# HGRN2 beside token projections: order of its small matmuls, banks of the projections, and norms of two banks at a time

## The chip, the cores and the metric

The kernel runs on one core of one Trainium2 chip, in one launch. The metric is the device time of an execution in microseconds (us); lower is better. Three runs of the kernel before were timed, and one further execution was profiled.

## The reference

A decoder trunk of two layers over 512 tokens of width 1024, all in float32. Each layer is a half-step SwiGLU, a mixing block and another half-step SwiGLU, each behind an RMS norm and added to the stream:

```python
for l in range(DEPTH):
    x = x + 0.5 * swiglu(rms_norm(x, ffn1_norm[l]), ffn1_w_in[l], ffn1_w_out[l])
    h = rms_norm(x, mix_norm[l]) @ w_mix_in[l]
    (c_x, c_b, c_c, h_q, h_f, h_i, h_g, f_q, f_k, f_v, f_f) = jnp.split(h, split_at, axis=-1)
    y = jnp.concatenate([
        short_conv_mixer(c_x, c_b, c_c, conv_w[l]),
        hgrn2_mixer(h_q, h_f, h_i, h_g, lower_bounds[l], hgrn_out_gain[l]),
        fox_mixer(f_q, f_k, f_v, f_f, fox_f_bias[l], fox_q_gain[l], fox_k_gain[l]),
    ], axis=-1)
    x = x + y @ w_mix_out[l]
    x = x + 0.5 * swiglu(rms_norm(x, ffn2_norm[l]), ffn2_w_in[l], ffn2_w_out[l])
```

The change lies in the HGRN2 mixer (4 heads of 64, chunks of 64 tokens) and in the projections and the query-key norm of the FoX attention (8 heads of 64). One chunk of HGRN2 is

```python
bcum = jnp.cumsum(lfb, axis=-2)
rel = bcum[..., :, None, :] - bcum[..., None, :, :]
decay = jnp.where(causal, jnp.exp(jnp.where(causal, rel, 0.0)), 0.0)
scores = jnp.einsum('bhtd,bhsd,bhtsd->bhts', qb, kb, decay)
o = (jnp.einsum('bhts,bhsv->bhtv', scores, vb)
     + jnp.einsum('bhtd,bhdv->bhtv', qb * jnp.exp(bcum), state))
b_last = bcum[..., -1:, :]
state = (jnp.exp(b_last[..., 0, :])[..., None] * state
         + jnp.einsum('bhsd,bhsv->bhdv', kb * jnp.exp(b_last - bcum), vb))
```

In FoX, query and key heads are each RMS-normed over their 64 columns before the attention.

## The kernel before

The large products are made of three passes of a split float32 (high times high, high times low, low times high; lines 312, 318 and 319 in the helper `mm3`). A weight granule (two blocks of 128 rows) is loaded by SP into `st`, ScalarE rounds it into the high part of `hl` (line 301), and VectorE takes the remainder (line 302); `st` has 2 buffers and `hl` 3. Accumulators are PSUM banks of 128 x 512, handed out by tag and by turns: 3 of "mm", 2 of "sc", 2 of "pt" and 1 of "po".

In a layer's mixing block, `mix`, the HGRN2 mixer is a generator (`hgrn`) whose stages are interleaved with the token projections of FoX (`fox_qkv`). Each `yield n` of `hgrn` lets n steps of the projections go, and a step is one granule: 24 matmuls of 128x256. There are six projections in that stream, of four steps each: Q, K and V of heads 0 to 3 (half 0), then Q, K and V of heads 4 to 7 (half 1). A projection fills two banks (four blocks of 128 tokens by 256 columns). The scheduler keeps the program's order on each engine except where priorities and dependencies say otherwise; each engine executes its own instructions in order, and waits on semaphores.

The stages of `hgrn`, with the lines of the profile:

- decays and gates on ScalarE and VectorE; keys decayed to the chunk's end, transposed (L1224) and copied (L1227);
- key-value products of all chunks (L1241), 64x64 matmuls into two "sc" banks, copied by ScalarE (L1248) beside the decay factors (L1252); VectorE scans the states S through the chunks (L1255);
- the diagonal of the scores and the first level (neighbouring tokens) as dots: e0 = q times k (L1273) and e1 (L1276, L1277, from an exponential of the odd columns of lf), summed over 64 rows by matmuls with a column of ones (the helper `scores`, L1264, called at L1280); they are spread into the score tile A with masks (L1283, L1286);
- the states' part of the output, 56 matmuls (L1298) into two "sc" banks, copied by ScalarE into `os` (L1309, L1313), which GpSimd zeroes for the first chunk (L1304);
- levels 2 to 6 in the groups (2, 3), (4, 5) and (6,): VectorE adds the references (L1327, L1328), ScalarE takes the exponential, VectorE multiplies by q (L1330), TensorE makes the scores (L1264), VectorE puts them into A by predicated copies (L1337);
- the values: A times v (L1353), the sum with `os` (L1359), and the output norm by a matmul of 128x512 with a block of ones (L1364).

After it come the decay sums of FoX (`fox_decay`, L1400), the convolution's projections and the attention, whose value products use the bank "po".

In `fox_qkv` each of a projection's two banks is normed by itself: ScalarE squares it (L1420), VectorE sums (L1421), scales (L1423), a reciprocal square root with one refining step (`rsqrt`, L399 to L401) and a last scaling (L1427) are done on 8 columns, and the product goes to `qk` (L1428). V is split into a high part (L1434) and a remainder (L1435). The banks are ("mm", "mm"), but ("mm", "po") for K of half 0.

## Time and profile before

| | |
|---|---|
| three timed runs | 1853.52 us median (1850.53 to 1854.43) |
| the profiled execution | 1851.91 us, of which the instructions span 1850.1 us |
| TensorE | 1819.1 us busy (98%) |
| VectorE | 1464.8 us busy (79%) |
| ScalarE | 994.8 us busy (54%) |
| mean granted TensorE clock | 0.999 |
| DMA | 250.94 MB, mean 136 GB/s |

PE is TensorE, PEld its weight load, DVE VectorE, ACT ScalarE, POOL GpSimd, SP the engine that issues most DMAs. Times in rows are us from the span's start, unless marked ns. Matmuls are pipelined, so the time from one start to the next is what a matmul takes from the engine, and it is shorter than the duration shown. Where a row ends in brackets, the engine was idle for so long before it, and what ended that time is named. The stage of the change is run twice, at about 398 to 482 us and 1308 to 1392 us.

### The profile page before, as it was taken

What the parts mean: (1) busy time and instruction counts of PE and PEld (TensorE: products, weight loads), DVE (VectorE), ACT (ScalarE), POOL (GpSimd) and SP (SyncE); (2) the same over time, 40 slices, a digit from 0 to 9 for tenths busy, and PEclk for the clock granted to TensorE, in tenths of its full rate; (3) what the DMA queues carried; (4) which work ended last, traced back from release to release, by engine and by line L of the source; (5) the groups of instructions that cost most, each with busy time, mean ns of one, the idle gap of its engine ahead of it and who ended that gap; (6) DMA issues with size and microseconds to landing.
All of it is one profiled execution on the core that took longest, in us unless ns stands there. A gap on an engine that the chain in (4) does not pass through costs nothing.

```text
span 1850.1 us, 34800 instructions
## 1 busy us (share of the span) xinstructions
PE 1819.1 (98%) x14328; PEld 1687.4 (91%) x14328; DVE 1464.8 (79%) x2047; ACT 994.8 (54%) x1427; POOL 169.1 (9%) x168
## 2 busy tenths in 40 slices
PE   8999999999999999999999999999999999999999
PEld 6799999899877899999889999998997788999997
DVE  7888887667797888879678887976768878888883
ACT  4455555454575555555445555554537664555552
POOL 0011120100000011112001111201000000020210
PEclk9999999999999999999999999999999999999999
DMA  7559684232323657868265797823223238677662
GB/s 205 162 117 200 170 175 101 74 87 71 81 75 98 205 128 169 191 174 171 78 186 136 161 191 193 164 69 81 76 76 87 75 92 228 148 160 194 147 139 91
DMA packets 244782, 250.94 MB, mean 136 GB/s; under 512 B 19440, under 2 KB 229872, under 8 KB 244624
## 3 DMA queue, kind: packets, MB, share of 16 engines
q1 hardware_dynamic: 191024, 182.64, 32.7%
q0 software_dynamic: 53600, 66.09, 22.4%
q8 instruction: 112, 1.84, 0.4%
q14 instruction: 46, 0.38, 0.1%
HBM read 223.98 MB, written 2.10 MB: 122 GB/s over the span
## 4 chain that ended last, share of the span: by engine, by line
PE 83%; DVE 9%; ACT 4%; issue 2%; DMA 2%; SPq 0%; ACTq 0%; DVEq 0%
PE mm L312 12%; PE mm L319 12%; PE mm L318 12%; PE sc L312 6%; PE sc L319 6%; PE sc L318 6%; PE pt L312 6%; PE pt L318 6%; PE pt L319 6%; PE po L318 3%; PE po L312 3%; PE po L319 3%; DVE hl L772 1%; DVE hl L302 1%; ACT hl L770 1%
## 5 line engine op out<-in xcount | busy, mean ns | idle before, releaser
L770 ACT CAST hl<-w 128x1024 fp32r<-128x1024 f32 x322 | 337.2, 1049 | 316.9 <-PE mm L319 74.9
L772 DVE TENSOR_TENSOR hl<-w,hl 128x1024 fp32r<-128x1024 f32 x322 | 392.8, 1222 | 93.0 <-ACT hl L770 93.0
L302 DVE TENSOR_TENSOR hl<-st,hl 128x512 fp32r<-128x512 f32 (+2 forms) x196 | 166.6, 852 | 125.8 <-ACT hl L301 124.3
L301 ACT CAST hl<-st 128x512 fp32r<-128x512 f32 (+2 forms) x196 | 146.4, 750 | 211.3 <-PE mm L319 82.4
L312 PE MATMUL mm<-xc,hl 128*128 128x256 f32 (+1 forms) x732 | 202.0, 277 | 1.8 <-ACT g L876 1.4
L319 PE MATMUL mm<-xc,hl 128*128 128x256 f32 x728 | 201.7, 277 | 0.5 <-DVE hl L772 0.5
L318 PE MATMUL mm<-xc,hl 128*128 128x256 f32 x728 | 201.5, 277 | 0.0
L312 PE MATMUL sc<-xc,hl 128*128 128x256 f32 (+1 forms) x530 | 146.7, 277 | 2.4 <-ACT g L876 1.7
L319 PE MATMUL sc<-xc,hl 128*128 128x256 f32 x528 | 146.5, 277 | 0.0
L318 PE MATMUL sc<-xc,hl 128*128 128x256 f32 x528 | 146.3, 277 | 0.0
L312 PEld LDWEIGHTS mm<-xc,hl 128*128 128x128 f32 x732 | 137.3, 188 | 2.7 <-ACT g L876 1.8
L319 PEld LDWEIGHTS mm<-xc,hl 128*128 128x128 f32 x728 | 136.9, 188 | 0.9 <-DVE hl L772 0.9
L318 PEld LDWEIGHTS mm<-xc,hl 128*128 128x128 f32 x728 | 136.7, 188 | 0.0
L312 PE MATMUL pt<-xc,hl 128*128 128x256 f32 (+1 forms) x484 | 133.2, 276 | 0.0
L318 PE MATMUL pt<-xc,hl 128*128 128x256 f32 x480 | 133.2, 277 | 0.0
L319 PE MATMUL pt<-xc,hl 128*128 128x256 f32 x480 | 132.9, 277 | 0.0
L312 PE MATMUL mm<-hl,x 128*128 128x256 f32 (+1 forms) x384 | 110.2, 287 | 4.4 <-DVE ft L399 2.8
L312 PE MATMUL mm<-x,hl 128*128 128x512 f32 x272 | 109.1, 401 | 0.7 <-ACT cy L1152 0.7
L318 PE MATMUL mm<-hl,x 128*128 128x256 f32 (+1 forms) x384 | 107.4, 280 | 0.0
L319 PE MATMUL mm<-x,hl 128*128 128x512 f32 x272 | 107.2, 395 | 0.0
L319 PE MATMUL mm<-hl,x 128*128 128x256 f32 (+1 forms) x384 | 107.0, 280 | 0.0
L318 PE MATMUL mm<-x,hl 128*128 128x512 f32 x272 | 106.9, 393 | 0.0
(481 smaller groups left out, 5602.1 us busy)
## 6 DMA issues: line engine op xcount, KB each, us to landing
w<-in_ffn_w_in_dram SPq DMA_DIRECT2D x140, 512.0 KB
w<-in_ffn_w_out_dram SPq DMA_DIRECT2D x64, 512.0 KB
w<-in_ffn_w_out_dram POOLq DMA_DIRECT2D x56, 512.0 KB, 9.5
st<-in_w_mix_in_dram SPq DMA_DIRECT2D x88, 256.0 KB
st<-in_ffn_w_in_dram SPq DMA_DIRECT2D x72, 256.0 KB
w<-in_ffn_w_in_dram POOLq DMA_DIRECT2D x35, 512.0 KB, 7.9
w<-S POOLq DMA_DIRECT2D x35, 512.0 KB, 4.7
st<-in_ffn_w_out_dram SPq DMA_DIRECT2D x24, 512.0 KB
```

Source lines behind the costliest of these rows:

```text
L301: a = nc.scalar.copy(hi, src[:, c : c + w])
L302: b = nc.vector.tensor_sub(lo, src[:, c : c + w], hi)
L312: i = nc.tensor.matmul(acc[:, c], ah, bh[:, c], start=first and c.start == 0, stop=False, skip_group_check=True,)
L318: nc.tensor.matmul(acc, ah, bl, start=False, stop=False, skip_group_check=True)
L319: i = nc.tensor.matmul(acc, al, bh, start=False, stop=last, skip_group_check=True)
L770: A(nc.scalar.copy(hi, src))
L772: return lambda: V(nc.vector.tensor_sub(lo, src, hi))
```

## The change

In `hgrn`, the matmuls of the dots are moved right behind those of the key-value products (with the making of e0 and e1 ahead of both), and the matmuls of the states right behind the scores of levels 2 and 3. The numbers of projection steps let through at each yield change from 1, 2, 2, 3, 3, 4, 4, 2, 2, 1 to 1, 2, 4, 5, 5, 3, 3, 1. In `fox_qkv`, the two banks of a Q or K projection are normed together: the squares and sums are made for each bank, the operations between are done once on 16 columns, and the two products follow. The second bank of a projection is "po" for K of half 0, Q of half 1 and V of half 1, and "mm" otherwise.

```diff
         nc.vector.tensor_mul(qe, qe, q)
         yield 2
 
-        U, dec, S = tmp(), tmp(), own("S", [P, 2, HD, NCH])
+        def scores(bank, at, held, moving, n):
...
+        A = own("A", [P, 2, 8, CH])
...
+        e0, e1 = tmp(), tmp()
+        nc.vector.tensor_mul(e0, q, k)
+        odd = half(e1, 1, 1)
+        self.act(odd, half(lf, 1, 1), AF.Exp)
+        nc.vector.tensor_mul(odd, odd, half(q, 1, 1))
+        nc.vector.tensor_mul(half(e1, 1, 0), odd, half(k, 1, 0))
         ub = [self.bank("sc") for _ in range(2)]
         for x in range(8):
...
                     v[rows[par], i, f], start=True, stop=True,
                 )
+        sb = [self.bank("pt") for _ in range(2)]
+        for at, e in ((8, e1), (0, e0)):
+            scores(sb, at, e, lambda r, c: self.ones_c[r, :], 1)
+        U, dec, S = tmp(), tmp(), own("S", [P, 2, HD, NCH])
...
         nc.vector.tensor_tensor_scan(
             S.rearrange("p r v c -> p (r v c)"), dec, U, 0.0, op0=ALU.mult, op1=ALU.add
         )
-        yield 2
-
-        def scores(bank, at, held, moving, n):
...
-        sb = [self.bank("pt") for _ in range(2)]
-        for at, e in ((8, e1), (0, e0)):
-            scores(sb, at, e, lambda r, c: self.ones_c[r, :], 1)
         for hh in range(2):
...
-        yield 3
-
-        ob = [self.bank("sc") for _ in range(2)]
...
+        yield 4
+
         os = own("lf", [P, W])
...
-        yield 3
-
-        for group, then in (((2, 3), 4), ((4, 5), 4), ((6,), 2)):
+
+        def states():
+            ob = [self.bank("sc") for _ in range(2)]
...
+        for group, then in (((2, 3), 5), ((4, 5), 5), ((6,), 3)):
...
             for at, lev, w, e, e2 in made[::-1]:
                 scores(sb, at, e, lambda r, c: e2[r, 32 * c : 32 * c + 32], 32)
+            if group[0] == 2:
+                states()
             for at, lev, w, e, e2 in made[::-1]:
...
         nc.scalar.activation(sq, o, AF.Square)
-        yield 2
+        yield 3
...
         for w, a in enumerate((F_Q, F_K)):
-            for bi, bank in enumerate((yield from tokens(a + 256 * hf, ("mm", "po" if w and not hf else "mm")))):
...
+            banks = yield from tokens(a + 256 * hf, ("mm", "mm" if w == hf else "po"))
+            s16 = lambda tag: mp.tile([P, 4, 4], F32, tag=tag, name=self.n(tag), bufs=2)
+            m, r, t = s16("fm"), s16("fr"), s16("ft")
+            bc = lambda c: c.unsqueeze(2).to_broadcast([P, 4, 4])
+            two = lambda bi: slice(2 * bi, 2 * bi + 2)
+            src = [x.rearrange("p (i h d) -> p i h d", i=2, h=4) for x in banks]
+            for bi in range(2):
+                out = qk[:, two(bi), :, w, :]
+                nc.scalar.activation(out, src[bi], AF.Square)
+                nc.vector.reduce_sum(m[:, two(bi)], out, axis=AX.X)
+            nc.vector.tensor_mul(m, m, bc(self.inv2))
+            self.act(r, m, AF.Ln, bias=self.epsc)
+            self.act(r, r, AF.Exp, scale=-0.5)
+            self.rsqrt(r, m, r, t)
+            nc.vector.tensor_mul(r, r, bc(self.invc))
+            for bi in range(2):
+                out = qk[:, two(bi), :, w, :]
+                nc.vector.tensor_mul(
+                    out, src[bi], r[:, two(bi)].unsqueeze(3).to_broadcast([P, 2, 4, HD])
+                )
         V = mp.tile([P, 4, 4, 2, HD], F32R, tag="V", name=self.n("V"), bufs=2)
-        for bi, bank in enumerate((yield from tokens(F_V + 256 * hf))):
+        for bi, bank in enumerate((yield from tokens(F_V + 256 * hf, ("mm", "po" if hf else "mm")))):
```

More of the change, by code (lines that the diff above doesn't have):

```diff
@@ L1233, in hgrn @@
         yield 2
-        U, dec, S = tmp(), tmp(), own("S", [P, 2, HD, NCH])
-        ub = [self.bank("sc") for _ in range(2)]
-        for x in range(8):
-            r, i = divmod(x, 4)
-            for par, hh in quarters:
-                f = slice(r * P + 64 * hh, r * P + 64 * hh + 64)
-                nc.tensor.matmul(
-                    ub[par][rows[hh], x * HD : (x + 1) * HD],
-                    span(kt, r)[rows[par], i * P + 64 * hh : i * P + 64 * hh + 64],
-                    v[rows[par], i, f], start=True, stop=True,
-                )
-        vc = lambda a: a.rearrange("p (r v c) -> p r v c", r=2, c=NCH)
-        for par in range(2):
-            nc.scalar.copy(
-                vc(U)[:, :, :, par::2], ub[par].rearrange("p (r i v) -> p r v i", r=2, i=4)
-            )
-        for r in range(2):
-            nc.scalar.copy(
-                vc(dec)[:, r], dc[:, r * NCH : (r + 1) * NCH].unsqueeze(1).to_broadcast([P, HD, NCH])
-            )
-        nc.vector.tensor_tensor_scan(
-            S.rearrange("p r v c -> p (r v c)"), dec, U, 0.0, op0=ALU.mult, op1=ALU.add
-        )
-        yield 2
         def scores(bank, at, held, moving, n):
@@ L1277, in hgrn @@
         nc.vector.tensor_mul(half(e1, 1, 0), odd, half(k, 1, 0))
+        ub = [self.bank("sc") for _ in range(2)]
+        for x in range(8):
+            r, i = divmod(x, 4)
+            for par, hh in quarters:
+                f = slice(r * P + 64 * hh, r * P + 64 * hh + 64)
+                nc.tensor.matmul(
+                    ub[par][rows[hh], x * HD : (x + 1) * HD],
+                    span(kt, r)[rows[par], i * P + 64 * hh : i * P + 64 * hh + 64],
+                    v[rows[par], i, f], start=True, stop=True,
+                )
         sb = [self.bank("pt") for _ in range(2)]
@@ L1280, in hgrn @@
             scores(sb, at, e, lambda r, c: self.ones_c[r, :], 1)
+        U, dec, S = tmp(), tmp(), own("S", [P, 2, HD, NCH])
+        vc = lambda a: a.rearrange("p (r v c) -> p r v c", r=2, c=NCH)
+        for par in range(2):
+            nc.scalar.copy(
+                vc(U)[:, :, :, par::2], ub[par].rearrange("p (r i v) -> p r v i", r=2, i=4)
+            )
+        for r in range(2):
+            nc.scalar.copy(
+                vc(dec)[:, r], dc[:, r * NCH : (r + 1) * NCH].unsqueeze(1).to_broadcast([P, HD, NCH])
+            )
+        nc.vector.tensor_tensor_scan(
+            S.rearrange("p r v c -> p (r v c)"), dec, U, 0.0, op0=ALU.mult, op1=ALU.add
+        )
         for hh in range(2):
@@ L1289, in hgrn @@
             )
-        yield 3
-        ob = [self.bank("sc") for _ in range(2)]
-        for x in range(8):
-            r, i = divmod(x, 4)
-            for hh, par in quarters:
-                c = 2 * i + par
-                if c:
-                    nc.tensor.matmul(
-                        ob[hh][rows[par], x * CH : (x + 1) * CH], S[rows[hh], r, :, c - 1],
-                        span(qe, r)[rows[hh], c * CH : (c + 1) * CH], start=True, stop=True,
-                    )
+        yield 4
         os = own("lf", [P, W])
@@ L1304, in hgrn @@
         nc.gpsimd.memset(os.rearrange("p (r t) -> p r t", r=2)[:, :, :CH], 0.0)
-        for hh in range(2):
-            for par in range(2):
-                out, src = chunk(os[rows[hh], :], par), C(ob[hh][rows[par], :])
-                if par:
-                    nc.scalar.copy(out, src)
-                else:
-                    for r in range(2):
-                        x = slice(4 * r + 1, 4 * r + 4)
-                        nc.scalar.copy(out[:, x, :], src[:, x, :])
-        yield 3
-        for group, then in (((2, 3), 4), ((4, 5), 4), ((6,), 2)):
+        def states():
+            ob = [self.bank("sc") for _ in range(2)]
+            for x in range(8):
+                r, i = divmod(x, 4)
+                for hh, par in quarters:
+                    c = 2 * i + par
+                    if c:
+                        nc.tensor.matmul(
+                            ob[hh][rows[par], x * CH : (x + 1) * CH], S[rows[hh], r, :, c - 1],
+                            span(qe, r)[rows[hh], c * CH : (c + 1) * CH], start=True, stop=True,
+                        )
+            for hh in range(2):
+                for par in range(2):
+                    out, src = chunk(os[rows[hh], :], par), C(ob[hh][rows[par], :])
+                    if par:
+                        nc.scalar.copy(out, src)
+                    else:
+                        for r in range(2):
+                            x = slice(4 * r + 1, 4 * r + 4)
+                            nc.scalar.copy(out[:, x, :], src[:, x, :])
+        for group, then in (((2, 3), 5), ((4, 5), 5), ((6,), 3)):
             sb = [self.bank("pt" if group[0] != 4 else "sc") for _ in range(2)]
@@ L1414, in fox_qkv @@
         for w, a in enumerate((F_Q, F_K)):
-            for bi, bank in enumerate((yield from tokens(a + 256 * hf, ("mm", "po" if w and not hf else "mm")))):
-                src = bank.rearrange("p (i h d) -> p i h d", i=2, h=4)
-                s8 = lambda tag: mp.tile([P, 2, 4], F32, tag=tag, name=self.n(tag), bufs=2)
-                out = qk[:, 2 * bi : 2 * bi + 2, :, w, :]
-                m, r, t = s8("fm"), s8("fr"), s8("ft")
-                nc.scalar.activation(out, src, AF.Square)
-                nc.vector.reduce_sum(m, out, axis=AX.X)
-                bc = lambda c: c[:, 2 * bi : 2 * bi + 2].unsqueeze(2).to_broadcast([P, 2, 4])
-                nc.vector.tensor_mul(m, m, bc(self.inv2))
-                self.act(r, m, AF.Ln, bias=self.epsc)
-                self.act(r, r, AF.Exp, scale=-0.5)
-                self.rsqrt(r, m, r, t)
-                nc.vector.tensor_mul(r, r, bc(self.invc))
-                nc.vector.tensor_mul(out, src, r.unsqueeze(3).to_broadcast([P, 2, 4, HD]))
+            banks = yield from tokens(a + 256 * hf, ("mm", "mm" if w == hf else "po"))
@@ L1429, in fox_qkv @@
+            nc.vector.tensor_mul(m, m, bc(self.inv2))
[7 more added lines that the diff above has]
+                    out, src[bi], r[:, two(bi)].unsqueeze(3).to_broadcast([P, 2, 4, HD])
+                )
         V = mp.tile([P, 4, 4, 2, HD], F32R, tag="V", name=self.n("V"), bufs=2)
-        for bi, bank in enumerate((yield from tokens(F_V + 256 * hf))):
+        for bi, bank in enumerate((yield from tokens(F_V + 256 * hf, ("mm", "po" if hf else "mm")))):
```

## The prediction

> **What bounds the kernel now.** I read the page first, then the list of waits of TensorE, then TensorE's timeline through the HGRN2 stage of layer 0 (398 to 482 us), the windows of the same stage in both layers, and the groups of VectorE there.

> ```profile
> span 1850.1 us, 34800 instructions
> PE 1819.1 (98%) x14328; PEld 1687.4 (91%) x14328; DVE 1464.8 (79%) x2047; ACT 994.8 (54%) x1427; POOL 169.1 (9%) x168
> ```

> TensorE is the bound: 98% busy, 31 us idle in all. A change that leaves its matmuls as they are can only win idle time, slow clock or start-up cost between matmuls. Three of TensorE's waits lie in the stage that is changed (the other rows of that list are lines of other stages):

> ```profile
> PE pt L1264 <- DVE ft L400: 2.9, 2, 1.5
> PE mm L312 <- DVE ft L399: 2.8, 4, 1.1
> PE mm L312 <- DVE V L1435: 1.6, 2, 0.8
> ```

> That is 7.3 us of idle time in two layers (columns: total, times, longest). The first is the wait of the two sets of one-column dots; the other two are token projections that want a bank whose reader on VectorE is not through. The names of the releasers are those that came last: for the dots what they really need is e1, two multiplications on VectorE just ahead. The timeline shows each place (columns: start, duration, engine, line, operation; in brackets the idle time before):

> ```profile
> 404.35 0.28 PE L319 MATMUL mm<-hl,x 128*128 128x256 f32 x1
> 404.56 1.16 PE L1241 MATMUL sc<-v,T 64*64 64x64 f32 x64
> 405.65 0.38 PE L312 MATMUL mm<-hl,x 128*128 128x256 f32 x1
> 405.87 0.29 PE L318 MATMUL mm<-hl,x 128*128 128x256 f32 x1
> ...
> 411.89 0.28 PE L312 MATMUL po<-hl,x 128*128 128x256 f32 x1
> 413.62 2.04 PE L1264 MATMUL pt<-ones_c,T 64*64 64x1 f32 x128 [1.45 <-DVE ft L400]
> ...
> 439.30 0.28 PE L319 MATMUL mm<-hl,x 128*128 128x256 f32 x1
> 439.41 0.28 PE L312 MATMUL mm<-hl,x 128*128 128x256 f32 x1
> 440.49 0.36 PE L312 MATMUL mm<-hl,x 128*128 128x256 f32 x1 [0.80 <-DVE V L1435]
> ...
> 467.76 1.14 PE L1353 MATMUL sc<-A,v 64*64 64x64 f32 x58
> 470.04 0.36 PE L312 MATMUL mm<-hl,x 128*128 128x256 f32 x1 [1.14 <-DVE ft L399]
> ...
> 471.62 0.34 PE L1353 MATMUL sc<-A,v 64*64 64x64 f32 x6
> 471.89 0.39 PE L312 MATMUL mm<-hl,x 128*128 128x256 f32 x1
> ```

> Windows of the stage (us, then busy time of PE, PEld, DVE, ACT, POOL, the granted clock, DMA share, GB/s): the dots, the state products, the first level scores, then a stretch of layer 1 and the 65 projection matmuls behind the dots in layer 0 and in layer 1.

> ```profile
> 413.62:415.59 1.97, 1.97 (x128) 1.96 (x128) 1.44 (x6) 0.07 (x1) 0.00 (x0) 1.00 0.13 30
> 423.44:425.52 2.08, 2.08 (x57) 2.01 (x57) 2.08 (x5) 1.64 (x4) 0.00 (x0) 1.00 0.40 122
> 433.89:435.89 2.00, 2.00 (x130) 1.96 (x129) 1.24 (x3) 0.62 (x1) 0.00 (x0) 1.00 0.51 139
> 1321.89:1325.30 3.41, 1.98 (x129) 2.00 (x129) 2.87 (x11) 1.37 (x5) 0.00 (x0) 1.00 0.41 95
> 1325.30:1328.72 3.42, 3.42 (x21) 3.42 (x17) 2.53 (x6) 0.00 (x0) 0.00 (x0) 0.50 0.19 63
> 415.59:423.44 7.85, 7.85 (x71) 7.72 (x65) 7.43 (x15) 3.28 (x5) 0.00 (x0) 1.00 0.26 68
> 1325.29:1334.47 9.18, 9.18 (x72) 9.05 (x66) 7.22 (x14) 3.08 (x5) 0.00 (x0) 0.81 0.19 55
> ```

> In layer 1 the clock stood at 0.50 for 3.42 us, right after 3.41 us that held nothing but the wait for the dots and the dots themselves. The same 65 matmuls took 9.18 us instead of 7.85: 1.33 us lost.

> **The change, part by part.**

> *Dots beside the key-value products.* The dots keep their number and stand right behind the products, where 55 projection matmuls lay between before. Their wait goes if e1 is ready when the products end, at 404.56 + 1.09 = 405.65. In the new order of VectorE, e0 comes right after the fox decay; ScalarE does the exponential of the odd columns right behind the two copies of the transposes; then two multiplications.

> ```profile
> 399.40 1.07 ACT L1227 COPY T<-pt 128x512 f32<-128x512 f32 x2
> L266 ACT ACTIVATE T<-lf 128x512 f32<-128x512 f32 x1 | 0.7, 694 | 0.0
> L1276 DVE TENSOR_TENSOR T<-T,q 128x512 f32<-128x512 f32 x1 | 0.7, 682 | 0.0
> ```

> Copies done at 400.47, exponential at 401.2, two multiplications of 0.68, one weight remainder between: e1 stands at about 402.7 and has 3 us in hand. If that cover were gone, each us of lateness is a us of TensorE, since nothing is queued between products and dots.

> *Norms of two banks, four banks by turns.* Before, the second bank of a projection is often the one its predecessor has just filled (Q of half 1 takes one of V's, K of half 1 one of Q's, V of half 1 one of K's, since the three "mm" banks go round). Now each of the six projections takes a pair other than the pair just filled, so a bank has a whole projection, 96 matmuls or about 11 us, to be read. The joint norm lets the first bank go later (it waits for the second's sum), by some 2 us of those 11. It saves 5 small operations on VectorE and 3 on ScalarE per projection, off the path. So I count both waits as gone, with nothing late behind them.

> The three waits are 7.3 us idle. As intervals they cost a little more. 439.41 to 440.49 is 1.08 us against 0.11 for an undisturbed matmul (439.30 to 439.41), so 0.97 where the bracket says 0.80. For the dots 1.73 against 0.21 for an undisturbed entry (404.35 to 404.56) is 1.52 against 1.45. For the last, 58 products in 2.28 us against 58/64 of 1.09 is 1.29 against 1.14. Taking the other "ft L399" wait of a layer like the first, the differences are 0.17 + 0.07 + 0.15 + 0.17 = 0.56 per layer: 7.3 + 1.1 = 8.4 us.

> *Fewer visits to small matmuls.* Each change from 128-wide matmuls to 64-wide ones and back costs: 0.21 - 0.11 on entry, 0.22 - 0.11 for the first matmul after (405.65 to 405.87), together 0.21; and the short visit of 6 took 0.27 where 6 at 1.09/64 are 0.10. So between 0.21 and 0.21 + 0.17 = 0.38; I take the middle, 0.29. Before there are 8 visits a layer (products, dots, states, three level groups, values twice), after it 5: dots join the products, states join the first levels, values are one run in the new order. 3 x 0.29 x 2 layers = 1.7 us.

> *The half clock in layer 1.* With the wait gone the window before it holds products and dots, 1.09 + 1.97 = 3.06 us, and at least 0.35 us of full matmuls, and no idle time. I take the 1.33 us as won. [...]

> *What is added: less cover for VectorE.* Between dots and first level scores there were 65 + 72 matmuls and the states; now 96 matmuls. TensorE is ready for the scores at 405.6 + 1.97 + 96 x 0.116 + 0.2 = 418.9 (0.116: 7.85 less 0.3 for two changes, over 65). VectorE has 20 instructions in that stretch in the new order:

> ```profile
> L302 DVE TENSOR_TENSOR hl<-st,hl 128x512 fp32r<-128x512 f32 x24 | 16.5, 689 | 20.2 <-ACT hl L301 20.2
> L1421 DVE TENSOR_REDUCE fm<-qk 128x8 f32<-128x512 f32 x8 | 5.4, 681 | 1.6 <-ACT qk L1420 1.6
> L1328 DVE TENSOR_TENSOR T<-b 128x512 f32<-128x512 f32 x5 | 3.5, 694 | 0.0
> L1255 DVE TENSOR_TENSOR_SCAN S<-T,T 128x1024 f32<-128x1024 f32 x1 | 2.3, 2291 | 0.8 <-ACT T L1252 0.8
> L1286 DVE COPY_PREDICATED A<-lmask,pt 128x256 f32<-128x256 uint8 x2 | 1.5, 734 | 0.0
> L1283 DVE TENSOR_TENSOR A<-ident,pt 128x512 f32<-128x512 f32 x2 | 1.4, 686 | 0.6 <-PE pt L1264 0.6
> L401 DVE TENSOR_TENSOR fr<-fr,ft 128x8 f32<-128x8 f32 x8 | 1.3, 165 | 0.2
> 418.55 0.69 DVE L302 TENSOR_TENSOR hl<-st,hl 128x512 fp32r<-128x512 f32 x1 [0.30 <-ACT hl L301]
> 419.16 0.68 DVE L1428 TENSOR_TENSOR qk<-mm,fr 128x512 f32<-128x512 f32 x1
> ```

> Back to back an operation of 0.69 takes 0.61 (418.55 to 419.16). Five exponents (L1327 and L1328 before), two identity products, two reductions, two remainders, two products with q are 13 x 0.61 = 7.9; the scan 2.2, two predicated copies 1.25, four small ones 0.4: 11.8 us. It begins when the first of the two sets of dots is done, 405.6 + half of 1.97 = 406.6, with 0.4 of waiting for the second set: 418.8. The two are level. I take a new wait of 0.2 a layer; between 0 and, with every operation at its full duration and no overlap, 1.5. Later groups have more: the next level operands are ready some 8 us before their scores. Queued behind a late operand there are only the scores, the states and the projections, all on TensorE.

> The state copies (L1309, L1313) move on ScalarE ahead of the second level group, and the fill on GpSimd moves up: same counts, off the path. The weight loads keep their order on SP, and come earlier with the buffers; DMA stands at 0.26 in 415.59:423.44.

> **Sum.** 8.4 + 1.7 + 1.3 - 0.4 = 11.0 us off the profiled execution, which took 1851.9 us (span 1850.1): 1840.9. The median of the three runs, 1853.5, is 1.6 above that execution and the fastest, 1850.5, is 1.4 below. I forecast 1841 us.

> **Rivals.**

> [...]

> *VectorE becomes the bound of the stage: slower.* The 20 instructions between dots and scores, and ScalarE's two exponentials within them, decide when the scores start, with the states and all later projections queued behind on TensorE. It costs from 11.8 us on, us for us, in both layers; at 17.3 us the gain is gone, and at 20 us, each exponent waiting for ScalarE in turn, the time is 1851.9 - 11 + 2 x 8.2 = 1857. Against: VectorE ran this kind of work back to back at 7.43 of 7.85 us (415.59:423.44).

> *The wait moves on: no change, 1851 to 1853.* The stage ends earlier, but the attention behind it, whose first value bank is now the last projection's "po", waits as long. Against: the decay products behind the output norm had no idle time of their own before, and the chain to them starts earlier with the values.

> **How the numbers follow.** Forecast 0.73; half clock 0.15, still faster by over 0.2%; no change 0.07; slower 0.05. 0.2% is 3.7 us, about what a measurement of this kernel can tell from no change. The range: from 1838.5 (no new wait, 0.4; visits at 0.38, 0.5; a run 1.4 below the profiled one) to 1846.5 (four half-clock drops, or a new wait of 1.5 a layer with the median 1.6 above the profiled run). It holds the first two cases. Faster 0.88, same 0.07, slower 0.05.

> **What would show it.** In the profile after: the dots follow the products with no idle time; the three waits above are missing; five visits a layer; a wait for an operand at the first level scores of at most 1.5 us; clock 1.00 throughout the stage; the stage shorter by about 5 us in layer 0 and 6 in layer 1, and the rest the same. Wrong would be a wait of over 5 us at the first scores, or new waits for banks in the attention.

## The result and the profile after

The changed kernel took 1845.2 us (median) against 1851.9 us before: ratio 0.9971, 95% interval [0.9959, 0.9984]. It is faster, by 6.7 us in the median and 5.4 by the ratio, where 11.0 were forecast. The same two kernels were measured in three more sets of rounds, each on its own:

| set | before | changed | ratio, 95% interval |
|---|---|---|---|
| 1 | 1851.9 | 1845.2 | 0.9971 [0.9959, 0.9984] |
| 2 | 1856.9 | 1842.7 | 0.9931 [0.9909, 0.9952] |
| 3 | 1856.2 | 1853.7 | 0.9983 [0.9970, 0.9996] |
| 4 | 1853.0 | 1844.4 | 0.9945 [0.9933, 0.9957] |

The gain in the medians is 6.7, 14.2, 2.5 and 8.6 us, by the ratios 5.4, 12.8, 3.2 and 10.2. These intervals do not all overlap, so something outside the change moves by more than the change's own error. The record lists another chip for each of sets 2, 3 and 4; whether the chip is what differs was not tested. The comparison of the profiles therefore goes by the stage, not by the span. First the page of the changed kernel and TensorE's waits:

```profile
span 1842.5 us, 34734 instructions
PE 1817.2 (99%) x14328; PEld 1686.7 (92%) x14328; DVE 1459.7 (79%) x2007; ACT 991.1 (54%) x1403; POOL 169.1 (9%) x168
```

```profile
PE sc L1301 <- issue: 1.8, 2, 0.9
PE pt L1239 <- issue: 1.1, 1, 1.1
```

The three waits of before ("pt L1264", "ft L399", "V L1435") are gone. In their place stand two new rows, with no releaser: "issue", in the states (L1301) and in the dots (L1239). (A third "issue" row, of 0.3 to 0.6 us in all, belongs to the attention and is in every profile, before as after.) The timeline shows where. Layer 0:

```profile
401.51 0.28 PE L319 MATMUL mm<-hl,x 128*128 128x256 f32 x1
401.72 1.16 PE L1258 MATMUL sc<-v,T 64*64 64x64 f32 x64
402.71 1.99 PE L1239 MATMUL pt<-ones_c,T 64*64 64x1 f32 x128
...
415.92 0.28 PE L319 MATMUL po<-hl,x 128*128 128x256 f32 x1
416.13 2.07 PE L1239 MATMUL pt<-e,T 64*64 64x32 f32 x128
418.02 2.12 PE L1301 MATMUL sc<-z,S 64*64 64x64 f32 x52
421.04 0.46 PE L1301 MATMUL sc<-z,S 64*64 64x64 f32 x4 [0.90 <-issue]
```

The dots follow the products with no idle time, and the first scores wait for nothing: both as forecast. But of the 56 state matmuls the last 4 come 0.90 us late, after 180 pairs of weight load and matmul in a row (128 + 52). Layer 1, where it happens twice, after 177 pairs (64 + 113) and after 144 (128 + 16):

```profile
1306.20 1.16 PE L1258 MATMUL sc<-v,T 64*64 64x64 f32 x64
1307.18 1.80 PE L1239 MATMUL pt<-ones_c,T 64*64 64x1 f32 x113
1310.06 0.41 PE L1239 MATMUL pt<-ones_c,T 64*64 64x1 f32 x15 [1.07 <-issue]
...
1321.52 2.07 PE L1239 MATMUL pt<-e,T 64*64 64x32 f32 x128
1323.38 0.94 PE L1301 MATMUL sc<-z,S 64*64 64x64 f32 x16
1325.19 1.54 PE L1301 MATMUL sc<-z,S 64*64 64x64 f32 x40 [0.87 <-issue]
```

As intervals the three cost 3.4 us: 421.04 - 418.02 = 3.02 for 52 matmuls that take 52/56 of 2.08 = 1.93 otherwise, 1.09 more; in the same way 1.14 (113 dots in 2.88) and 1.22 (16 state matmuls in 1.81). The windows of the stage, from the first transpose to the decay products, before (first two rows) and after (us, busy time of PE, clock, DMA share, GB/s):

```profile
398.14:483.43 85.29, 81.69 (x1204) 1.00 0.29 76
1307.84:1394.09 86.25, 82.52 (x1203) 0.98 0.29 75
```

```profile
395.10:475.65 80.55, 79.62 (x1204) 1.00 0.32 80
1299.78:1382.51 82.73, 80.77 (x1203) 1.00 0.30 78
```

Layer 0 is 4.74 us shorter (about 5 forecast), layer 1 is 3.52 shorter (about 6 forecast): 8.3 of 11.0. I call the sum of both stages the stage time: 171.5 us before, 163.3 after. It is what the experiments below are compared by. It is taken from one profile a run, and it is not free of two things that the change does not set: windows at half clock, and a slower pace of the 128x256 matmuls (below), which took 2.3 us of the 171.5 and 2.4 of the 163.3.

### The profile page after: what moved, and what is told of

It is laid out like the page before. It is cut to its first block, busy times and chain, and to the rows that moved or that the text cites. A ratio compares the mean times of both kernels' runs of the same rounds, so it can differ in the third digit from the quotient of the medians.

```text
span 1842.5 us, 34734 instructions
## 1 busy us (share of the span) xinstructions
PE 1817.2 (99%) x14328; PEld 1686.7 (92%) x14328; DVE 1459.7 (79%) x2007; ACT 991.1 (54%) x1403; POOL 169.1 (9%) x168
## 4 chain that ended last, share of the span: by engine, by line
PE 87%; DVE 6%; ACT 3%; issue 2%; DMA 1%; SPq 0%; ACTq 0%
PE mm L312 13%; PE mm L319 12%; PE mm L318 12%; PE sc L312 6%; PE sc L319 6%; PE sc L318 6%; PE pt L312 6%; PE pt L318 6%; PE pt L319 6%; PE po L312 4%; PE po L318 4%; PE po L319 3%; DVE hl L302 1%; DVE hl L772 1%; PE po L1504 1%
## 5 line engine op out<-in xcount | busy, mean ns | idle before, releaser
L302 DVE TENSOR_TENSOR hl<-st,hl 128x512 fp32r<-128x512 f32 (+2 forms) x196 | 166.4, 851 | 121.0 <-ACT hl L301 119.5
L301 ACT CAST hl<-st 128x512 fp32r<-128x512 f32 (+2 forms) x196 | 146.5, 749 | 208.0 <-PE po L319 81.7
L312 PE MATMUL mm<-xc,hl 128*128 128x256 f32 (+1 forms) x732 | 201.7, 276 | 1.8 <-ACT g L876 1.4
L319 PE MATMUL mm<-xc,hl 128*128 128x256 f32 x728 | 201.4, 277 | 0.0
L318 PE MATMUL mm<-xc,hl 128*128 128x256 f32 x728 | 201.3, 277 | 0.0
L312 PE MATMUL sc<-xc,hl 128*128 128x256 f32 (+1 forms) x530 | 146.8, 278 | 2.5 <-ACT g L876 1.7
L319 PE MATMUL sc<-xc,hl 128*128 128x256 f32 x528 | 146.6, 278 | 0.0
L318 PE MATMUL sc<-xc,hl 128*128 128x256 f32 x528 | 146.4, 277 | 0.0
L312 PEld LDWEIGHTS mm<-xc,hl 128*128 128x128 f32 x732 | 137.3, 188 | 2.5 <-ACT g L876 1.8
L318 PEld LDWEIGHTS mm<-xc,hl 128*128 128x128 f32 x728 | 136.8, 188 | 0.0
L319 PEld LDWEIGHTS mm<-xc,hl 128*128 128x128 f32 x728 | 136.7, 188 | 0.1
L312 PE MATMUL pt<-xc,hl 128*128 128x256 f32 (+1 forms) x484 | 133.4, 277 | 0.0
L318 PE MATMUL pt<-xc,hl 128*128 128x256 f32 x480 | 133.2, 278 | 0.0
L319 PE MATMUL pt<-xc,hl 128*128 128x256 f32 x480 | 133.0, 277 | 0.0
L312 PE MATMUL mm<-x,hl 128*128 128x512 f32 x272 | 108.9, 401 | 0.7 <-ACT cy L1152 0.7
L319 PE MATMUL mm<-x,hl 128*128 128x512 f32 x272 | 107.6, 396 | 0.0
L318 PE MATMUL mm<-x,hl 128*128 128x512 f32 x272 | 106.7, 392 | 0.0
L312 PEld LDWEIGHTS sc<-xc,hl 128*128 128x128 f32 x530 | 99.5, 188 | 3.3 <-ACT g L876 2.1
L319 PEld LDWEIGHTS sc<-xc,hl 128*128 128x128 f32 x528 | 99.6, 189 | 0.1
L318 PEld LDWEIGHTS sc<-xc,hl 128*128 128x128 f32 x528 | 99.2, 188 | 0.0
```

Of the source, the lines that this page charges most:

```text
L301: a = nc.scalar.copy(hi, src[:, c : c + w])
L302: b = nc.vector.tensor_sub(lo, src[:, c : c + w], hi)
L312: i = nc.tensor.matmul(acc[:, c], ah, bh[:, c], start=first and c.start == 0, stop=False, skip_group_check=True,)
L318: nc.tensor.matmul(acc, ah, bl, start=False, stop=False, skip_group_check=True)
L319: i = nc.tensor.matmul(acc, al, bh, start=False, stop=last, skip_group_check=True)
```

## Experiments

My theory was one of **supply**: that TensorE's instructions come in pieces, and that a long run of small pairs uses them up faster than they come. It was a guess, from one row of the page and the places of the stalls:

```profile
q8 instruction: 112, 1.84, 0.4%
```

In the trace each of the 112 packets has 16,384 bytes. What they carry no row says; if it is TensorE's 14328 loads and 14328 matmuls, they hold 28,656 / 112 = 255.9 instructions each, by my estimate 256, that is 128 pairs of weight load and matmul. The two stalls of layer 1 fit such a grid: their visits start 289 pairs apart, and 289 + 144 = 433 = 177 + 2 x 128. Rivals: an **operand** or a bank that is late, and nothing but the **pace** and clock of TensorE, which vary from run to run.

**Move the grid (e_shift).** In each layer 24 extra one-column matmuls, which show as 48 pairs, ahead of the transposes, whose results the transposes overwrite:

```
             tb = self.bank("pt")
+            if r == 0:
+                for i in range(24):
+                    nc.tensor.matmul(
+                        tb[:64, i : i + 1], lf[:64, 64 * (i % 8) : 64 * (i % 8) + 64],
+                        self.ones_c[:64, :], start=True, stop=True,
+                    )
```

> The changed kernel with 24 matmuls of one column (48 pairs, 96 instructions of TensorE) put ahead of the transposes in each layer, into a bank that the transposes then overwrite. They leave every wait as it was, but move all later instructions of TensorE by 96 in layer 0 and by 192 in layer 1. Supply theory, with pieces of 256 instructions (128 pairs) that are fetched one after the other: the stall of the states of layer 0 moves from pair 180 of its visit to about pair 132, now at the seam of the first scores and the states; a new stall comes up in the dots of layer 0 at about pair 165 of products and dots; in layer 1 the stall of the dots goes, and that of the states moves from pair 144 to about pair 176. Operand theory: all three stalls stay at the instructions where they are. Time: the 48 pairs cost 0.7 us and a longer visit in each layer, so about 1.5 us and one stall more than the changed kernel.

Timeline, products and dots (a), scores and states (b) of layer 0, then the same of layer 1:

```profile
407.69 1.16 PE L1264 MATMUL sc<-v,T 64*64 64x64 f32 x64
408.67 1.63 PE L1245 MATMUL pt<-ones_c,T 64*64 64x1 f32 x101
411.27 0.62 PE L1245 MATMUL pt<-ones_c,T 64*64 64x1 f32 x27 [0.97 <-issue]
...
424.80 0.43 PE L1307 MATMUL sc<-z,S 64*64 64x64 f32 x4
426.28 1.90 PE L1307 MATMUL sc<-z,S 64*64 64x64 f32 x52 [1.05 <-issue]
...
1319.60 1.99 PE L1245 MATMUL pt<-ones_c,T 64*64 64x1 f32 x128
...
1334.52 1.91 PE L1307 MATMUL sc<-z,S 64*64 64x64 f32 x48
1336.77 0.47 PE L1307 MATMUL sc<-z,S 64*64 64x64 f32 x8 [0.34 <-issue]
```

Pair 64 + 101 = 165, pair 128 + 4 = 132, no stall in the dots of layer 1, pair 128 + 48 = 176: all four as the supply theory had it. A stall that moves by the number of instructions ahead of it is no wait for an operand. The trace holds the packets of q8 one by one. Each of the 20 stalls of this kind in the stage, in the eight profiles that have them, ends 1.2 to 1.5 us after a packet has landed: in the changed kernel's first, a packet moves from 418.80 to 419.73 and TensorE goes on at 421.04, 1.31 us later; in layer 1 packets land at 1308.62 and 1323.71, and it goes on 1.44 and 1.48 us later. The number of packets rises with TensorE's instructions too, 113 for the 96 pairs more of this run. The waits of 0.3 us in the attention do not follow a packet so (in the same profile they end 20.9 and 3.8 us after the last one); what ends them is not shown. The time, 1848.8 us, was missed: the 48 pairs, all in one quarter of the array, took 2.96 us a layer and not 0.7, and each layer had a window at half clock behind them.

**Part the long visits (e_split, e_split2).** One projection step between products and dots, one between first scores and states:

```
+        yield 1
         sb = [self.bank("pt") for _ in range(2)]
...
-        yield 4
+        yield 3
...
-            if group[0] == 2:
-                states()
...
+            if group[0] == 2:
+                yield 1
+                states()
+                then = 4
             yield then
```

> The changed kernel with the two long visits parted again: one step of a projection (24 matmuls) between the products and the dots, and one between the first level scores and the states, so that no visit has more than 128 pairs of weight load and matmul. Supply theory: all three stalls go, 3.4 us less, and two more visits a layer cost 4 x 0.29 = 1.2 us: 2.2 us faster than the changed kernel in the same rounds (ratio 0.9988), and states and dots take 1.97 us for 128 pairs in both layers. Operand theory: the stalls stay, at the states above all, and the kernel is 1.2 us slower than the changed one, less what the 2.7 us of matmuls in between hide. Pace theory: no stall was a matter of place, the kernel is 1.2 us slower.

> The parted version again. Stalls and clock theory: no stall without a releaser, mean clock of the runs 0.999 or more, and a mean time 2 to 4 us below that of the changed kernel in the same rounds (2.2 to 3.4 us of stalls and 1 half-clock window of 1.7 us, less 1.2 for two visits a layer and 2 x 0.6 for the wait at the first scores). Pace theory: the mean lies within 2 us of the changed kernel's, on either side.

No stall without a releaser in the stage of either profile. The stage (e_split), its wait, and the two rows that price it:

```profile
394.30:474.69 80.39, 79.55 (x1203) 1.00 0.30 80
1298.91:1379.31 80.40, 79.56 (x1204) 1.00 0.30 80
```

```profile
PE pt L1239 <- DVE e L1330: 1.6, 2, 0.8
```

```profile
404.93 2.04 PE L1239 MATMUL pt<-ones_c,T 64*64 64x1 f32 x128
...
416.62 0.56 PE L1239 MATMUL pt<-e,T 64*64 64x32 f32 x25 [0.82 <-DVE e L1330]
```

Stage time 160.8 in both runs of it, 1.8 to 3.4 below four profiles of the changed kernel (163.3, 162.6, 164.2, 162.6), although it has two visits a layer more and a wait that I had not foreseen: with 76 matmuls between dots and scores, instead of 96, VectorE is late. In time it was level with the changed kernel in set 2 (0.9934 [0.9911, 0.9956] against 0.9931), where 2.2 us were expected, and 2.4 us ahead of it in the mean of set 4 (1841.5 against 1843.9; ratios 0.9935 [0.9923, 0.9946] and 0.9945), where the intervals still overlap.

**States beside level 6 (e_l6), and with one step more ahead of the first scores (e_late).** The edit is `if group[0] == 6: states()` with the dots one step behind the products; in e_late the steps go 4, 5, 4, 3 instead of 3, 5, 5, 3.

> The states beside the scores of level 6 (64 + 56 = 120 pairs in one visit) instead of beside those of levels 2 and 3, and the dots one projection step behind the products: one visit a layer more than the changed kernel, and none over 128 pairs. Supply theory: no stall without a releaser in the stage; 3.4 - 2 x 0.29 = 2.8 us faster than the changed kernel in the same rounds (ratio 0.9985). Operand theory: the scan has long ended by then, so that the stall of the states goes (1.8 us in two layers) and that of the dots stays in part; 1.2 us faster. Pace theory: 0.6 us slower, and nothing to be seen at these places.

> The version with the states beside level 6 and the dots one step behind the products, with one step more between dots and first level scores (96 matmuls instead of 76) and one less between levels 2/3 and 4/5. In the version with 76 the first scores waited 0.82 us in each layer. If that wait is the 11 to 12 us of VectorE between dots and scores, 20 matmuls of 0.113 (2.3 us) take it away, and the span of the profile is 1.6 us shorter than 1835.3, about 1833.7. If the wait hangs on ScalarE or on a bank of the level before, it stays and the span with it. Stalls without a releaser: none by the supply theory. Against the kernel before: 0.992 to 0.995; against the changed kernel in the same rounds 2 to 4 us faster where the pace allows to see it.

No such stall in the stage of either; stage time 160.1 and 159.7. In e_late the wait of 0.82 us is gone in both layers, which fits the 11 us or so of VectorE. Its layer 1 took 79.0 us, its layer 0 80.8 with a half-clock window behind the dots. By ratio they were 0.9945 [0.9924, 0.9966] (set 2, where the changed kernel had 0.9931, so the 2.8 us expected of e_l6 do not show in time) and 0.9955 [0.9938, 0.9972] (set 3, against 0.9983); the span of e_late, 1845.1, missed 1833.7 for a reason outside the stage (two slow stretches of 4.4 us, below).

**The changed kernel again (a_again, a_2, a_3).**

> The changed kernel once more, nothing edited. Supply theory: the three stalls of TensorE without a releaser (one in the states of layer 0, 0.90 us; one in the dots and one in the states of layer 1, 1.07 and 0.87 us) come back at the same instructions with the same length within 0.2 us, since they hang on the place of the instructions in the program. Operand theory (the states wait for a copy or the scan, the dots for a bank): they may come back too, but move with VectorE and ScalarE. Pace theory (what is missing of the gain is only the pace at which the 128x256 matmuls run, and half-clock windows): the total of slow stretches changes by several us from one profile to the next, and with it the time; the time against the kernel before lies between 0.994 and 0.999.

> The changed kernel a third time, beside the parts of it. Against the kernel before in the same rounds: 0.9931 to 0.9971 (the two ratios so far). Stalls without a releaser: in the dots of layer 1 at pair 177 for certain, in the states of layer 0 at pair 180 for certain, in the states of layer 1 at pair 144 in one of two profiles so far, so even odds.

> The changed kernel in the same rounds as the three below. Ratio to before: between 0.9931 and 0.9983, as in the three sets so far. Mean granted clock of its runs 0.9983 to 0.9985 as before; that of the kernel before 0.9973.

With the first profile that makes four. The stall in the dots of layer 1 at pair 177 came four times (1.1, 1.1, 1.7, 1.1 us), that in the states of layer 0 at pair 180 four times (0.9, 1.2, 0.9, 0.7), that in the states of layer 1 at pair 144 only in the first. Stalls per profile: 3, 2, 2, 2. So a_again missed the third stall that the supply theory expected, and the even odds for it in a_2 were too high. The packets show why: in the first profile the one in question started 73 pairs into the visit, in the other three 8 to 24 pairs into it, and little or nothing was left to wait for. The ratio of a_2, 0.9983, lies outside the 0.9931 to 0.9971 that I expected.

**The two halves of the change alone (e_hgrn, e_banks).** New hgrn with old fox_qkv, and the reverse.

> Only the first half of the change: the new order of dots and states, with the old projections (three banks by turns in part, norms of each bank by itself). By the steps of the prediction: the wait of the dots goes (2 x 1.52 us) with the half clock of layer 1 (1.3), the waits of the projections for banks stay (0.97 and twice 1.29 in each layer before). Since states and values are then dealt out in two pieces each, visits are 6 or 7 instead of 8. Supply theory: the stalls of the changed kernel stay (184 and 192 pairs in a row), 2 to 3 us. Sum: 3.0 + 1.3 + 0.6 - 2.5 = 2.4 us faster than before, ratio about 0.9987. If the order is worth the most of the change: 0.995.

> Only the second half of the change: projections over four banks by turns and joint norms, with the old order of dots and states. By the steps of the prediction: the waits of the projections for banks go (2 x (0.97 + 2 x 1.29) = 7.1 at most, 5.4 by the idle time in the list of waits without the dots), the values are one run (0.3 to 0.4 a layer), the wait of the dots stays (1.5 us a layer) with the risk of the half clock. Sum: 5 to 6 us faster than before, ratio about 0.997. Supply theory: no stall without a releaser, since no visit is over 128 pairs. If the banks are not what is waited for, the waits turn up at the next releaser and the ratio is 1.000.

```profile
PE mm L312 <- DVE fr L401: 2.0, 2, 1.0
PE pt L1239 <- issue: 1.5, 1, 1.5
PE sc L1301 <- issue: 1.5, 1, 1.5
```

```profile
PE pt L1264 <- DVE T L1277: 2.9, 2, 1.5
```

The first three rows are e_hgrn, the last e_banks. Stage time 171.2 for the new order alone (three half-clock windows in layer 1) and 163.5 for the banks alone: 0.4 and 8.1 us below before. In e_banks the idle time of the stage fell from 3.60 + 3.73 us to 1.49 + 1.46, by 4.4 us, just the forecast idle time of the two waits; the other 3.7 us are busy time, of which start-up behind the waits and values in one run were to be 1.0 and 0.6. The rest is pace: over the stage the starts of the 128x256 matmuls beyond 113.3 ns apart add up to 2.27 us before and 0.45 here, 1.8 less.

```profile
396.88:477.92 81.04, 79.55 (x1204) 1.00 0.31 80
1306.39:1388.83 82.44, 80.98 (x1204) 0.98 0.30 78
```

The new order was worth next to nothing by its stage, since 3 us of stalls and the clock took what it won. In time the two came out the other way round, 0.9970 [0.9955, 0.9985] where 0.9987 was expected, and 0.9991 [0.9978, 1.0004] where 0.997 was, with 7.0 and 11.1 us of slow pace in their profiles. That the banks are worth more than the order is thus shown by the stage of one profile each, and not by the times.

**Early operands without long visits (e_early, e_early2), and with the new banks (e_both).** The kernel before, with the four instructions of e0 and e1 moved ahead of the products; e_both has the new fox_qkv as well. Every visit stays by itself.

> The kernel before with one edit: the five instructions that make the operands of the dots stand ahead of the products, as in the changed kernel; the dots themselves stay where they were, 48 matmuls behind the products. By the prediction: the wait of the dots goes in both layers (1.5 us each), nothing takes its place, and the other waits stay. Supply theory: no stall without a releaser, since no visit is over 128 pairs. [...] Span of the profile, less slow pace and half clock: 3 us shorter than that of before (1843.6), about 1840.5.

> The kernel before with the operands of the dots made early and nothing else. The profile of it so far, less slow pace, was 4 to 5 us shorter than that of before, and had no half-clock window, where those of before had one and three. Expected: 3.0 us for the waits and up to 2.9 windows of 1.7 us of the mean clock of before (0.9973): 4 to 7 us faster than before, ratio 0.996 to 0.998, mean clock 0.999 or more. If the half clock of before does not hang on the wait of the dots, the mean clock stays at 0.9973 and the ratio is 0.9985.

> The kernel before with the operands of the dots made early and with the new projections, but the old order of visits: products, dots, states, three groups of levels, values each by themselves, none over 128 pairs. All three waits gone, no stall, no long visit. Against the changed kernel: 2 visits a layer more (1.2 us), no stalls (2.2 to 3.4) and no half clock from long visits (0 to 3): 1 to 5 us faster in the same rounds; span of the profile less slow pace and half clock about 1833, against 1834 to 1836 of the changed kernel's three profiles. If the long visits cost nothing in the timed runs, it is 1.2 us slower.

The stage of e_both:

```profile
396.98:476.48 79.50, 79.48 (x1203) 1.00 0.32 81
1301.27:1380.77 79.50, 79.48 (x1204) 1.00 0.32 81
```

In 79.50 us TensorE is idle for 0.02. Stage time 159.0, 12.5 below before (1.6 of it slow pace) and 3.6 to 5.2 below the changed kernel. In the same rounds: e_both 1839.1 us, ratio 0.9922 [0.9910, 0.9934]; the changed kernel 1844.4, 0.9945 [0.9933, 0.9957]; e_early2 1846.3, 0.9963 [0.9951, 0.9974]. So e_both beats both kernels, by 5.3 us the changed one, and its slowest run (1840.4) is ahead of the fastest of the changed kernel (1841.0). Moving four instructions alone (stage time 166.1 and 167.9) won 6.7 us in these rounds, more than the 3.0 of its waits: the mean granted clock rose with it from 0.9973 to 0.9993, two windows of half clock a run, 1.33 us each.

**What lowers the clock (b_again, e_ones3).** The kernel before again, and e_split with the dots issued three times over.

> The kernel before once more, for a second profile of it. [...] The waits of the dots (1.5 us), of L399 and of V come back within 0.2 us. The pace of the 128x256 matmuls changes in stretches of 114 us, each 4.4 us dearer or not at all.

> The parted version (no visit over 128 pairs) with the dots issued three times over, so that 384 pairs of one column stand in a row in each layer, with no operand to wait for. Clock by columns (a window filled with one-column matmuls counts as idle although TensorE is busy): the clock stands at 0.50 for at least one window of 3.41 us right behind, or in, the dots of both layers. Clock by idleness: it stays at 1.00, since TensorE is never idle there. Supply theory: after the first 128 pairs or so the pairs come at the rate of the fetch, 128 pairs per 3.2 to 3.4 us instead of 1.97, with two stalls of about 1.1 us in each layer, near pairs 252 and 380 in layer 0 and 218 and 346 in layer 1; the visit takes 8.0 to 8.5 us and not 5.9. Operand theory: 5.9 us without a gap.

b_again had three half-clock windows, two behind the dots of layer 0 and one behind those of layer 1 (stage time 174.2). e_ones3:

```profile
407.77 4.41 PE L1239 MATMUL pt<-ones_c,T 64*64 64x1 f32 x253
412.84 4.10 PE L1239 MATMUL pt<-ones_c,T 64*64 64x1 f32 x131 [0.66 <-issue]
```

```profile
407.51:410.92 3.41, 3.41 (x219) 3.28 (x220) 3.41 (x4) 1.23 (x3) 0.00 (x0) 1.00 0.05 12
410.92:414.34 3.42, 2.76 (x106) 2.67 (x105) 1.58 (x4) 1.68 (x4) 0.00 (x0) 0.50 0.32 81
```

```profile
1322.32 3.42 PE L1239 MATMUL pt<-ones_c,T 64*64 64x1 f32 x218
1326.96 3.59 PE L1239 MATMUL pt<-ones_c,T 64*64 64x1 f32 x128 [1.21 <-issue]
1330.70 1.24 PE L1239 MATMUL pt<-ones_c,T 64*64 64x1 f32 x38 [0.16 <-issue]
```

A window in which TensorE was busy for 3.41 of 3.41 us, with one-column matmuls, was followed by one at 0.50, and three windows in each layer stood at 0.50. The visit of layer 0 took 9.1 us (8.0 to 8.5 expected), with one stall at pair 253 (252 was expected, and 380, where none came) and the rest at half clock. Layer 1 (last three rows) stalled at pairs 218 and 346, both as expected, the second for only 0.16 us. How few columns a window had before the clock fell can be read from two profiles of the same kernel, e_early2 (first two rows) and e_early:

```profile
409.05:412.46 3.41, 3.41 (x142) 3.27 (x141) 3.41 (x11) 2.60 (x7) 0.00 (x0) 1.00 0.32 84
412.46:415.87 3.41, 3.41 (x19) 3.41 (x18) 3.34 (x10) 0.50 (x3) 0.00 (x0) 0.50 0.29 77
```

```profile
408.96:412.37 3.41, 3.41 (x141) 3.40 (x140) 3.41 (x12) 2.88 (x8) 0.00 (x0) 1.00 0.33 84
412.37:415.78 3.41, 3.41 (x32) 3.41 (x31) 3.41 (x10) 0.64 (x2) 0.00 (x0) 1.00 0.29 77
```

The dropped window had all 128 dots and 11 of the 256-column matmuls started in it, the other 120 dots and 13. In e_late 11 dropped it too; in e_split (both layers, layer 0 below) and e_l6 12 did not. A window of them alone holds 30, at 113.3 ns each.

```profile
403.55:406.97 3.42, 3.42 (x142) 3.28 (x141) 2.67 (x2) 2.34 (x5) 0.00 (x0) 1.00 0.25 73
406.97:410.38 3.41, 3.41 (x31) 3.41 (x31) 3.41 (x7) 0.43 (x1) 0.00 (x0) 1.00 0.30 82
```

So idle time is not what these windows have in common: the clock stood at 0.50 after windows that TensorE spent fully busy (3.41 of 3.41 us in e_ones3, e_early2 and e_late). The columns moved tell them apart better, 2,944 in the window of e_early2 that was followed by half clock against 3,448 in that of e_early. That is my reading of these windows; what sets the clock is not shown. By this reading the wait of the dots before was dear twice over, and a stall within the dots is again: a_again, a_2 and a_3 had 1, 2 and 1 half-clock windows behind the dots of layer 1. Columns alone are not the whole of it: one window of e_hgrn, with a stall of 1.48 us and 3,328 columns in small matmuls (49 of 64 and 6 of 32), was followed by half clock, where one of e_split with 3,200 (12 of 256 and 128 of 1) was not. Over the runs of a set the mean granted clock was 0.9973 before, 0.9983 to 0.9988 for the changed kernel, 0.9993 and 0.9994 for e_split, 0.9996 for e_both. One window of 3.41 us at half clock takes 0.0009 off that mean.

**The pace far from the change (e_whole).** The 128x256 matmuls run at two paces, 113.3 and 117.7 ns from start to start, at clock 1.00 both. In the FFN the first matmul of twelve products (my expectation says eight) is made in two halves of 128 columns, and the pace often changes there. The edit takes the halves away:

```
-                kind == "I" and p == "P1" and w in (covered, *(f0 for f0, _ in CHUNKS)),
+                False,
```

> The changed kernel with one edit far from the change: in the FFN the first matmul of eight of the products runs over 256 columns in one piece instead of two of 128. In the profiles so far each of these eight places is a flip of the pace of the 128x256 matmuls: 117.8 ns from start to start ahead of it became 113.4 to 113.7 behind it each time, and 113.3 ahead of it became in some profiles 117.8 for the whole stretch of 114 us behind it (4.4 us each), in others not; the granted clock is 1.00 in both. Pace theory (the two halves are what flips it): without them no stretch behind one of these places begins slow where the one ahead was fast; the 4.4 us steps go, the runs lie closer together than 16 us, and the median is 2 to 8 us below that of the changed kernel (1842.7 to 1853.7 in three sets of rounds), ratio to before 0.990 to 0.995. If the pace is set by something else (weights from memory, the place in the instruction stream), stretches of 4.4 us still come, and ratio and spread stay as they were. A slow stretch that enters one of these places would then no longer be ended by it.

The same stretch of the FFN in a_again, then in the changed kernel's first profile; behind them one stretch of e_whole:

```profile
1590.00:1700.00 110.00, 110.00 (x972) 1.00 0.77 182
```

```profile
1590.00:1700.00 110.00, 110.00 (x936) 1.00 0.76 175
```

```profile
680.00:790.00 110.00, 110.00 (x936) 1.00 0.74 168
```

My expectation had it the wrong way round: without the halves the kernel was slower than before, 1.0036 [1.0009, 1.0062], with runs from 1851 to 1876 us. A slow stretch then goes on, 260 us in one piece (640 to 900), over places where the halves ended it in the other profiles, and its profile has about 22 us of slow pace. In the 17 other profiles, at the three places that follow other work (near 680, 1010 and 1590 us), the halves were reached at the slow pace 28 times and left at the fast one 28 times; they were reached at the fast pace 23 times and left at the slow one 8 times, for the next 114 us and some 1000 matmuls: 4.4 us each time. The profile of the changed kernel had one such stretch (1588 to 1706 us), that of before none, and a smaller sort ahead of the halves (0.9 us each, three of them). Slow pace took 5.0 and 6.0 us in the profiles of before, 3.1 to 8.0 in four of the changed kernel. What chooses between the two at a place reached fast is open; no run here tells it. The edit also took 3 matmuls out ahead of the stage of layer 0 and 9 ahead of that of layer 1, and the stalls came 3 and 9 pairs later in their visits (183, 186 and 153 where the changed kernel has 180, 177 and 144): the grid again.

## Why the prediction was right or wrong

1. *The dots' wait:* right. e1 was ready when the products ended, in both layers, and nothing took the place of the wait.
2. *The banks:* right, and not too high. The waits are gone; 5.4 us of intervals and 0.6 for the values were in the sum, and e_banks alone shortened the stage by 8.1 us, 4.4 of them idle time as forecast and 1.8 pace, which is not the banks' doing; 6.3 are left.
3. *Fewer visits, 1.7 us won:* **this step failed, in its sign.** It priced a visit by its entry and exit (0.29) and took what lies in it to go on at the pace of a short one. The two merges, seven visits of e_both against five, did not save 2 x 2 x 0.29 = 1.2 us but cost 3.6 to 5.2 us of stage time. Less slow pace and half clock (1.7 us a window) the cost is 1.5 to 2.5. The price of an entry and exit itself was about right: e_l6, with one visit a layer fewer than e_split, has a stage time 0.7 us shorter, where 2 x 0.29 were forecast. What the step left out are the stalls that I put down to supply, 3.4 us in the first profile, which no visit of before showed; none was longer than 128 pairs. Its visits of 192 and 184 pairs follow from counts that I had, and no row of the trace had such a length; I put no bound on it.
4. *Half clock, 1.33 us won:* half right. The stage of the changed kernel's first profile had clock 1.00 in both layers. The half clock was more frequent than I had it: before it hit layer 0 too (two windows in b_again), and with early operands it was rarer (mean clock 0.9973 to 0.9993). But behind the merged dots of layer 1, in which TensorE had stalled for 1.1 to 1.7 us, it was back in three of the four profiles of the changed kernel. So the half clock to which I gave 0.15 was at work, by 1.7 us a window. Behind the long visit of scores and states the clock fell only in e_hgrn, after a window that held a stall of 1.48 us.
5. *VectorE between dots and scores, 0.4 us lost:* nothing was lost in the changed kernel. In e_split the first of the two sets of dots ended at about 404.93 + 1.0 = 405.95, and the scores began at 416.62: 10.7 us where I had summed 11.8 and 0.4 for waiting. The rival by which VectorE becomes the bound needs 12 and more; e_split, with 20 matmuls less, shows how near it is, and with the old norms (e_hgrn) the first scores of layer 0 waited 1.1 us for VectorE.
6. *The sum:* in the stage 8.3 us of 11.0. The 2.7 us that are missing are the 3.4 of stalls, less the 0.4 that VectorE did not cost and 0.3 that I can't place. Taken together the other terms hold, and the failed step accounts for the gap. "The rest the same" was wrong as a statement on single executions: the start was 3.0 us shorter and the end 4.0 longer. The end has the slow stretch of 4.4 us in it; what set the start is not shown. It differs by 1.6 to 1.7 us between profiles of one kernel.

The median of 1845.2 us lies inside the range of 1838.5 to 1846.5, and this is luck: its upper end was drawn for half-clock drops and for a wait on VectorE, not for stalls, nor for a slow stretch in the FFN.

What stays open is how much of the 6.7 us of the first set is the change and how much the pace of that set. The four sets give 2.5 to 14.2. The stage times give 7.3 to 9.0 against the first profile of before, and 10.0 to 11.7 against the second, which had two more windows at half clock; pace alone is 0.8 to 2.4 us of each of these stage times.

## What to carry to other kernels

Merging visits of small matmuls saved the change of shape as long as a visit held no more pairs than a packet of q8 by my estimate (120 in e_l6, against 128); visits of 184 and more stalled (20 times in eight profiles, 0.2 to 1.7 us), and lengths between were not run. For a longer visit, count what TensorE is fed, and put wide matmuls between. Bring the operands forward before you move the consumer: four instructions moved ahead, with every visit left alone, shortened the stage by 3.7 to 5.5 us; the whole new order without the new banks did so by 0.4, with three windows at half clock. And where whole runs scatter by more than the change is worth, compare the stage between two fixed instructions over several profiles, and take clock and pace out first.
